# A Trainium2 transformer layer: x^T's first blocks issued from ScalarE's queue, and the first projection chunk run product by product

## The chip, the cores and the metric

The kernel runs on one core of a Trainium2 chip. The metric is the device time of the whole kernel in microseconds (us), the median of several runs. TensorE (PE) does the matrix products, ScalarE (ACT), VectorE (DVE) and GpSimd (POOL) the element work, and DMAs are issued from SyncE's queue (SP) and here, after the change, from ScalarE's queue as well.

## The reference

One layer of a decoder on 256 tokens of width 1024, all in float32: one input projection to 3072 columns, rotary on the first 16 of each head's 64 dims, differential attention (4 heads) and causal attention (8 heads; with 256 tokens the block-sparse group has only its own block), an output projection, LayerNorm, a SwiGLU feed-forward of width 2816, and a second LayerNorm.

```
proj = x @ w_in                              # 256x1024 @ 1024x3072
a = diff_attention(rope(dq), rope(dk), dv);  b = moba_attention(rope(mq), rope(mk), mv)
x = layer_norm(ALPHA * x + concat(a, b) @ w_o)
g, u = split(x @ w_ffn_in)
x = layer_norm(ALPHA * x + (silu(g) * u) @ w_ffn_out)
```

## The kernel before

Every float32 operand of a weight product is split into two parts, hi and lo, and a product runs as three matmuls into one PSUM bank: hi times x's hi, hi times x's lo, lo times x's hi (`mm3`, lines 132 to 134). The weights come as a stream of 1 MB units of four blocks of 128 x 512 (`load_unit`, line 85). ScalarE copies each piece to its hi part (line 96), VectorE subtracts to get the lo part (line 98); of units 2 to 9, GpSimd does one lo piece in four. Five raw buffers, four hi and four lo buffers turn over; x^T's raw tile takes one of the five.

Chunks 0 to 3 of the input projection (`proj_qkT`) give q^T and k^T of the two attention groups, chunks 4 and 5 give the values. Chunk 0 is four column blocks j of 128 columns, each with its own PSUM tile `pj0_j`, over eight contraction blocks k. Its loop runs over k outside and j inside, and each (j, k) is one `mm3`. The four results then go through `rope` (lines 235 to 245), whose shuffles, products and splits are done by VectorE, GpSimd and ScalarE while chunk 1 runs on TensorE. Scores (`scores`, line 271), the combination of the two softmaxes (`diff_combine`, line 296) and transposes (`diff_pt`) are woven into chunks 2 and 3 in the same manner.

At the start, seven matmuls on zeros (`WARM`, line 144) run while the first loads are on their way. x^T (8 blocks of 128 x 256, 128 KB each) and the first unit of w_in (4 blocks of 256 KB) are loaded by eight DMAs, all from SyncE's queue, in an order written by hand (lines 161 and 164); then units 1 to 3 follow in pieces of 256 KB. Each block is split as it arrives (lines 168, 169, 180, 182). The framework that builds the program sorts the instructions of each engine by its own estimate of when they can run, so that the order on an engine is not always that of the source.

Of the kernel before, what the change touches and what calls it, by code (L numbers as in the profile page):

```python
# [11 lines left out]
F32 = mybir.dt.float32  # L12
F32R = mybir.dt.float32r
BF16 = mybir.dt.bfloat16
AF = mybir.ActivationFunctionType
ALU = mybir.AluOpType

P = 128
S = 256
D = 1024  # L20
KT = D // P
# [8 lines left out]
EPS = 1e-5  # L30
WARM = 7  # matmuls on zeros that raise the tensor engine's clock while the first loads run

# weight units loaded / split in more pieces than usual: unit -> pieces
LOAD_PIECES = {1: 4, 2: 4, 3: 4, 4: 4, 5: 4, 6: 2, 7: 2}
SPLIT_PIECES = {16: 4, 17: 4, 18: 4, 19: 4}

# steps of a projection chunk at which attention work is woven in
FIN0, FIN1, FIN2, FIN3 = (20, 24, 28, 31), (4, 6, 8, 10), (5, 4), (5, 2)
SCORES0, SCORES1 = (18, 22, 26, 30), (3, 5, 7, 9)
COMBINE, DIFF_PT = 12, (22, 25, 28, 31)  # L40

# partner of each rotary dim within a 32-partition quadrant
SWAP = [(i + HALF) % 16 if i < 16 else i for i in range(32)]


# The 256 tokens are one key block of the block-sparse group: there is no past block to select, so
# its softmax runs over the own block under the causal mask.
# Weight products: every float32 operand is split exactly into two float32r parts (12 bits each), and
# hi*hi + hi*lo + lo*hi accumulate in PSUM.


@with_exitstack
def hybrid_layer_kernel(ctx, tc, xT, xr, w_in, w_o, w_f1, w_f2, cols, rows, lamb, rot, tri, out):
    nc = tc.nc
# [8 lines left out]

# [1 line left out]
    # unit: [128, 4 blocks, 512] float32, split into two float32r parts  # L65
    units = []
# [11 lines left out]
    raw, hi, lo = {}, {}, {}  # L78
# [26 lines left out]
    def spread(units_, pieces, steps):  # L105
        """Hooks that emit the split of some units evenly over a number of steps."""
        gens = [(u, p) for u in units_ for p in range(pieces)]
        live = {}

        def emit(u):  # L110
            if u not in live:
                live[u] = split_gen(u, pieces)
                state["split"] = u + 1
            next(live[u])

        hooks = {}
        for i, (u, p) in enumerate(gens):
            hooks.setdefault(i * steps // len(gens), []).append(lambda u=u: emit(u))
        return hooks
# [15 lines left out]

# [1 line left out]
    warm = const.tile([P, 512], BF16, name="warm")  # L137
    nc.vector.memset(warm, 0.0)
    tbl = const.tile([P, 2], F32, name="tbl")
    nc.vector.memset(tbl, 0.0)  # L140
    nc.scalar.activation(tbl[:, 1:2], tbl[:, 0:1], AF.Exp)
    wps = psB.tile([P, 512], F32, tag="b", name="wps")
# [16 lines left out]

    def load_x(a, b):  # L160
        nc.sync.dma_start(xTr[:, a:b, :], xT[:, a:b, :])

    def load_w0(i):
        nc.sync.dma_start(raw[0][:, i, :], units[0][:, i, :])

    def split_x(a, b, copy=nc.scalar.copy):
        s = slice(a, b)
        copy(xTh[:, s, :], xTr[:, s, :])  # L168
        nc.vector.tensor_sub(xTl[:, s, :], xTr[:, s, :], xTh[:, s, :].bitcast(F32))

    load_w0(0)
    load_x(0, 1)
    load_x(1, 2)
    load_w0(1)
    load_x(2, 4)
    load_w0(2)
    load_w0(3)
    load_x(4, 8)
    for i in range(4):
        nc.scalar.copy(hi[0][:, i, :], raw[0][:, i, :])  # L180
        split_x(i, i + 1, nc.vector.tensor_copy if i == 0 else nc.scalar.copy)
        nc.vector.tensor_sub(lo[0][:, i, :], raw[0][:, i, :], hi[0][:, i, :].bitcast(F32))
# [23 lines left out]

# [1 line left out]
    apool = axT.enter_context(tc.tile_pool(name="apool", bufs=1))  # L208
    V = [apool.tile([P, 2, 512], F32, name=f"V{i}") for i in range(2)]
    # per pair of 128-row blocks: first token tile in float32, the rest in two float32r parts  # L210
    F0, QH, QL, SH, QA = {}, {}, {}, {}, {}
# [14 lines left out]
    def rope(c, js, ps):  # L226
        """128-row blocks js of q^T or k^T, PSUM -> SBUF, with the rotary part applied."""
        b, m = js[0] // 2, len(js)
        if js[0] % 2 == 0:
            qk_tiles(c, b)  # L230
            SH[c, b] = rpool.tile([P, 2, S], F32, tag="sh", name=f"sh{c}_{b}", bufs=2)
            QA[c, b] = rpool.tile([P, 2, S], F32, tag="qk", name=f"a{c}_{b}", bufs=2)
        bs = slice(js[0] % 2, js[0] % 2 + m)
        sh, a = SH[c, b][:, bs, :], QA[c, b][:, bs, :]
        nc.vector.stream_shuffle(sh, ps, SWAP)
        nc.vector.tensor_mul(a, ps, cos2[:, :m, :])
        nc.gpsimd.tensor_mul(sh, sh, sin2[:, :m, :])
        f, h, l = F0[c, b][:, bs, :], QH[c, b][:, bs, :], QL[c, b][:, bs, :]

        def finish():  # L240
            nc.vector.tensor_add(a, a, sh)
            src = a if c % 2 else a[:, :, P:]
            nc.scalar.copy(h, src)
            nc.vector.tensor_sub(l, src, h.bitcast(F32))
            nc.scalar.copy(f, a[:, :, :P])

        return finish
# [40 lines left out]
    def diff_combine():  # L288
        """E_c0 - lam * (l0 / l1) * E_c1, per query row."""
        sc = small.tile([P, 2, 4], F32, tag="sc", name="sc")  # L290
# [76 lines left out]

# [1 line left out]
    def proj_tok(ps, c, t, k):  # L369
# [4 lines left out]
    def proj_qkT(c, side):  # L374
        """One 512-column chunk, transposed: 128 columns on the partitions, 256 tokens."""
        pool, tag = (psB, "b") if c == 1 else (psA, "acc")
# [5 lines left out]
        bg = spread([1] + [2] if c == 0 else [3, 4, 5] if c == 1 else [2 * c + 2, 2 * c + 3], 4, 28)  # L382
        for n, (j, k) in enumerate(order):
            if n == 16:
# [20 lines left out]
    def proj_v(c, side):  # L405
        """One 512-column chunk for both token tiles."""
        pss = [psA.tile([P, 512], F32, tag="acc", name=f"pj{c}_{t}") for t in range(2)]
# [43 lines left out]

# [1 line left out]
    acc = [[psA.tile([P, 512], F32, tag="acc", name=f"wo{t}_{n}") for n in range(2)] for t in range(2)]  # L453
# [93 lines left out]

# [1 line left out]
    hp = ctx.enter_context(tc.tile_pool(name="hp", bufs=1))  # L549
# [5 lines left out]
    def glu_store(sl, h):  # L555
        """h (float32) -> both parts of h^T."""
        nc.scalar.copy(hTh[sl], h)
        nc.vector.tensor_sub(hTl[sl], h, hTh[sl].bitcast(F32))

    def ffn_rows(c, t, mid=()):  # L560
        """Chunk with tokens on the PSUM partitions; then transposes."""
        ps = psB.tile([P, 512], F32, tag="b", name=f"fr{c}_{t}")
# [54 lines left out]

# [1 line left out]
    acc2 = [[psA.tile([P, 512], F32, tag="acc", name=f"fo{t}_{n}") for n in range(2)] for t in range(2)]  # L619
# [108 lines left out]
```

## Time and profile before

| | |
|---|---|
| median of 3 runs | 319.07 us (318.89 to 320.75) |
| span of the profiled execution, first to last instruction | 317.0 us |
| mean granted TensorE clock | 0.993 of full |
| busy share of the span | PE 96%, PE's weight loads 82%, DVE 71%, ACT 53%, POOL 11% |
| moved by DMA | 57.18 MB, mean 180 GB/s |

The span leaves out what lies before the first and behind the last instruction; the profiled execution has no time of its own beside it, and the median is 2.1 us more than the span. A busy share is an average over the whole span: which engine sets the pace has to be read stretch by stretch. A matmul's record is longer than the distance to the next one, since matmuls are pipelined, so TensorE's speed is read from the distance of two starts.

### The profile page before, as it was taken

The page shows a single profiled execution, that of the slowest core. Times are in us where ns is not written, and L with a number is a line of the kernel's source. Part 1 is how long each engine was busy: PE and PEld are TensorE (multiplying, and loading weights), DVE is VectorE, ACT ScalarE, POOL GpSimd, SP SyncE. Part 2 cuts the span into 40 slices and gives each one's busy share as a digit, 9 for nine tenths or more (in the row PEclk, how much of TensorE's full clock was granted, in tenths as well). Part 3 has the DMA queues.
Part 4 walks back from the last instruction along what each step waited for, and adds up shares of the span by engine and source line. Part 5 has one row for each costly group of instructions (what it writes and reads, how often), then busy time and mean ns, then how long its engine had stood idle before and what let it go on. Part 6 is the DMA issues. An engine that isn't in the chain of part 4 may idle for free.

```text
span 317.0 us, 4689 instructions
## 1 busy us (share of the span) xinstructions
PE 304.6 (96%) x1741; PEld 259.7 (82%) x1741; DVE 224.4 (71%) x437; ACT 169.0 (53%) x349; POOL 36.1 (11%) x38
## 2 busy tenths in 40 slices
PE   7999899999999999999999999999999999999990
PEld 4999789867887788888888888888888888888880
DVE  3799999999977389949386577658657753343275
ACT  3757489398685328247467547646754642422000
POOL 1076553310030010100000000000000000000011
PEclk9999999999999999999999999999999999999997
DMA  6999963444376442659654574475357474000011
GB/s 176 377 305 375 423 236 134 132 135 147 125 254 213 188 136 74 212 247 309 220 172 142 218 254 136 142 267 167 141 224 254 144 266 132 0 2 0 0 66 67
DMA packets 12310, 57.18 MB, mean 180 GB/s; under 512 B 1504, under 2 KB 2272, under 8 KB 6784
## 3 DMA queue, kind: packets, MB, share of 16 engines
q1 hardware_dynamic: 12000, 54.79, 49.5%
q0 software_dynamic: 288, 2.10, 1.9%
q8 instruction: 13, 0.21, 0.3%
q14 instruction: 9, 0.07, 0.1%
HBM read 55.84 MB, written 1.05 MB: 179 GB/s over the span
## 4 chain that ended last, share of the span: by engine, by line
PE 77%; DVE 12%; DMA 4%; issue 3%; POOL 1%; ACT 1%; SPq 1%; DVEq 0%; ACTq 0%
PE fc L590 21%; PE fc L591 11%; PE fo L134 6%; PE fo L132 6%; PE fo L133 6%; DMA raw<-in_w_in_dram 4%; DVE lo L98 4%; PE wo L132 2%; PE fr L133 2%; PE fr L132 2%; PE wo L134 2%; PE wo L133 2%; PE fr L134 2%; PE pj L132 2%; PE pj L134 2%
## 5 line engine op out<-in xcount | busy, mean ns | idle before, releaser
L98 DVE TENSOR_TENSOR lo<-raw,hi 128x1024 fp32r<-128x1024 f32 (+1 forms) x122 | 118.2, 995 | 41.2 <-ACT hi L96 41.1
L96 ACT CAST hi<-raw 128x512 fp32r<-128x512 f32 (+1 forms) x130 | 100.5, 824 | 38.3 <-PE fo L134 19.2
L590 PE MATMUL fc<-x1T,hi 128*128 128x512 f32 x288 | 100.1, 392 | 0.0
L591 PE MATMUL fc<-x1T,lo 128*128 128x256 f32 x288 | 80.7, 280 | 0.0
L590 PEld LDWEIGHTS fc<-x1T,hi 128*128 128x128 f32 x288 | 54.1, 188 | 11.8
L591 PEld LDWEIGHTS fc<-x1T,lo 128*128 128x128 f32 x288 | 54.1, 188 | 0.0
L132 PE MATMUL pj<-xTh,hi 128*128 128x256 f32 x128 | 37.1, 296 | 1.0 <-DVE xTh L168 0.9
L134 PE MATMUL pj<-xTh,lo 128*128 128x256 f32 x128 | 36.2, 289 | 0.7 <-DVE lo L98 0.5
L133 PE MATMUL pj<-xTl,hi 128*128 128x256 f32 x128 | 36.6, 287 | 0.0
L132 PE MATMUL fo<-hi,hTh 128*128 128x512 f32 x82 | 32.4, 395 | 0.0
L133 PE MATMUL fo<-lo,hTh 128*128 128x512 f32 x82 | 32.4, 395 | 0.0
L134 PE MATMUL fo<-hi,hTl 128*128 128x512 f32 x82 | 32.4, 395 | 0.0
L132 PEld LDWEIGHTS pj<-xTh,hi 128*128 128x128 f32 x128 | 24.6, 195 | 2.6 <-ACT hi L180 2.1
L134 PEld LDWEIGHTS pj<-xTh,lo 128*128 128x128 f32 x128 | 24.4, 194 | 1.3 <-DVE lo L98 0.7
L594 DVE TENSOR_TENSOR v<-v,fc 128x256 f32<-128x256 f32 x36 | 15.0, 418 | 14.5 <-ACT v L593 14.5
L133 PEld LDWEIGHTS pj<-xTl,hi 128*128 128x128 f32 x128 | 25.0, 195 | 0.0
L593 ACT COPY v<-fc 128x256 f32<-128x256 f32 x36 | 13.3, 370 | 20.8 <-PE fc L591 20.7
L505 POOL TENSOR_TENSOR rsf<-rsf,mhalf 128x1 f32<-128x1 f32 x2 | 1.8, 924 | 179.3 <-DVE rsf L504 179.3
L134 PEld LDWEIGHTS fo<-hi,hTl 128*128 128x128 f32 x82 | 15.5, 189 | 3.6
L133 PEld LDWEIGHTS fo<-lo,hTh 128*128 128x128 f32 x82 | 15.5, 189 | 3.6
L132 PEld LDWEIGHTS fo<-hi,hTh 128*128 128x128 f32 x82 | 15.5, 189 | 3.5
L98 POOL TENSOR_TENSOR lo<-raw,hi 128x512 fp32r<-128x512 f32 x8 | 13.5, 1689 | 21.3 <-ACT hi L96 21.3
(148 smaller groups left out, 455.8 us busy)
## 6 DMA issues: line engine op xcount, KB each, us to landing
raw<-in_w_f_dram SPq DMA_DIRECT2D x33, 1024.0 KB, 5.2
raw<-in_w_in_dram SPq DMA_DIRECT2D x24, 256.0 KB, 5.4
raw<-in_w_in_dram SPq DMA_DIRECT2D x4, 1024.0 KB, 10.1
raw<-in_w_o_dram SPq DMA_DIRECT2D x4, 1024.0 KB, 4.8
raw<-in_w_in_dram SPq DMA_DIRECT2D x4, 512.0 KB, 7.9
rows<-in_rows_dram POOLq DMA_DIRECT2D x2, 1024.0 KB, 6.9
x_sb<-in_xr_dram SPq DMA_DIRECT2D x1, 1024.0 KB, 10.5
out_dram<-z SPq DMA_DIRECT2D x3, 256.0 KB, 2.1
```

Of the source, the lines that this page charges most:

```text
L96: nc.scalar.copy(h[:, s, :], r[:, s, :])
L98: eng.tensor_sub(l[:, s, :], r[:, s, :], h[:, s, :].bitcast(F32))
L132: nc.tensor.matmul(ps, sh, mh, start=first, stop=False)
L133: nc.tensor.matmul(ps, sh, ml, start=False, stop=False)
L134: nc.tensor.matmul(ps, sl, mh, start=False, stop=last)
L505: nc.gpsimd.tensor_tensor(rs, rs, mhalf[:, :1], op=ALU.pow)
L590: nc.tensor.matmul(ps, hi[u][:, i, ws], x1T[:, k], start=k == 0, stop=False)
L591: nc.tensor.matmul(ps[:, 0, :], lo[u][:, i, ws], x1T[:, k, 0, :], start=False, stop=k == KT - 1)
L593: nc.scalar.copy(v, ps[:, 1, :])
L594: nc.vector.tensor_add(v, v, ps[:, 0, :])
```

## The change

- `WARM` goes from 7 to 9.
- x^T's blocks 0 and 1 are issued from ScalarE's queue, ahead of the first `Exp` that loads its table; the rest stays on SyncE's queue.
- The first weight block is loaded as two halves of 256 columns, and its hi part is made in two halves too.
- The start's splits are written in another order: for block 0, x^T's split on VectorE stands around the weight's; for blocks 1 to 3, x^T's split stands ahead of the weight's.
- Chunk 0 runs, for each k, one product over all four column blocks, then the next product, in place of the three products of one column block after another.

```diff
-WARM = 7  # matmuls on zeros that raise the tensor engine's clock while the first loads run
+WARM = 9
...
-    nc.scalar.activation(tbl[:, 1:2], tbl[:, 0:1], AF.Exp)
...
-    load_w0(0)
-    load_x(0, 1)
-    load_x(1, 2)
+    load_x(nc.scalar, 0, 1)
+    load_x(nc.scalar, 1, 2)
+    nc.scalar.activation(tbl[:, 1:2], tbl[:, 0:1], AF.Exp)
+    load_w0(0, 0, 256)
+    load_w0(0, 256, 512)
     load_w0(1)
-    load_x(2, 4)
+    load_x(nc.sync, 2, 4)
     load_w0(2)
     load_w0(3)
-    load_x(4, 8)
-    for i in range(4):
+    load_x(nc.sync, 4, 8)
+    nc.vector.tensor_copy(xTh[:, 0, :], xTr[:, 0, :])
+    nc.scalar.copy(hi[0][:, 0, :256], raw[0][:, 0, :256])
+    nc.vector.tensor_sub(xTl[:, 0, :], xTr[:, 0, :], xTh[:, 0, :].bitcast(F32))
+    nc.scalar.copy(hi[0][:, 0, 256:], raw[0][:, 0, 256:])
+    nc.vector.tensor_sub(lo[0][:, 0, :], raw[0][:, 0, :], hi[0][:, 0, :].bitcast(F32))
+    for i in range(1, 4):
+        split_x(i, i + 1)
         nc.scalar.copy(hi[0][:, i, :], raw[0][:, i, :])
-        split_x(i, i + 1, nc.vector.tensor_copy if i == 0 else nc.scalar.copy)
         nc.vector.tensor_sub(lo[0][:, i, :], raw[0][:, i, :], hi[0][:, i, :].bitcast(F32))
...
-        for n, (j, k) in enumerate(order):
+        for k in range(KT if c == 0 else 0):
+
+            u, i = k // 4, k % 4
+            for p, (w, x) in enumerate(((hi, xTh), (hi, xTl), (lo, xTh))):
+                if 4 * k + p == 16:
+                    ahead(1, splits=-1)
+                for f in bg.get(4 * k + p, []) + (bg.get(4 * k + 3, []) if p == 2 else []):
+                    f()
+                for j in range(4):
+                    nc.tensor.matmul(pss[j][:, 0, :], w[u][:, i, j * P : (j + 1) * P], x[:, k, :],
+                                     start=(k, p) == (0, 0), stop=(k, p) == (KT - 1, 2))
+        for n, (j, k) in enumerate(order if c else ()):
```

On SyncE's queue (SP) the start's DMAs stood in this order before (xTr is x^T, raw_101 the first weight unit, raw_139 the next; the sizes are partitions x elements):

```order
L164 DMA raw_101<-in_w_in_dram 128x512
L161 DMA xTr<-in_xT_dram 128x256 x2
L164 DMA raw_101<-in_w_in_dram 128x512
L161 DMA xTr<-in_xT_dram 128x512
L164 DMA raw_101<-in_w_in_dram 128x512 x2
L161 DMA xTr<-in_xT_dram 128x1024
L85 DMA raw_139<-in_w_in_dram 128x512 x4
```

and stand in this one now (raw_102 is the first weight unit, raw_143 the next):

```order
L160 DMA xTr<-in_xT_dram 128x512
L163 DMA raw_102<-in_w_in_dram 128x256 x2
L163 DMA raw_102<-in_w_in_dram 128x512 x3
L160 DMA xTr<-in_xT_dram 128x1024
L85 DMA raw_143<-in_w_in_dram 128x512 x4
```

The built order differs from the source's: x^T's blocks 2 and 3 (128 x 512) have moved to the head of SyncE's queue, ahead of all weights, while blocks 0 and 1 are on ScalarE's queue.

ScalarE's first instructions now (before, it had the table load, the activation, and then casts of weights and x^T in turn, a weight first):

```order
L160 DMA xTr<-in_xT_dram 128x256 x2
L172 ACT_TABLE_LOAD
L172 ACTIVATE tbl<-tbl 128x1
L167 CAST xTh<-xTr 128x256 x2
L181 CAST hi_103<-raw_102 128x256
L167 CAST xTh<-xTr 128x256
L183 CAST hi_103<-raw_102 128x256
L187 CAST hi_103<-raw_102 128x512 x3
```

The two issues stand ahead of the table load, and the first weight cast stands behind the casts of x^T's blocks 1 and 2.

On VectorE, some 50 us into the program, where the last score block (s_3) is turned into E and the combination of the softmaxes (`sc`, then eight products into E) follows, before:

```order
L235 STREAM_SHUFFLE sh_1_744<-pj_1_520 128x512
L236 TENSOR_TENSOR a_1_745<-pj_1_520,cs_sb 128x512
L98 TENSOR_TENSOR lo_754<-raw_521,hi_753 128x512
L241 TENSOR_TENSOR a_1_745<-a_1_745,sh_1_744 128x512
L291 RECIPROCAL rl_518<-ls_517 128x16
L292 TENSOR_TENSOR sc<-ls_517,rl_518 128x8
L98 TENSOR_TENSOR lo_754<-raw_521,hi_753 128x512
L244 TENSOR_TENSOR l_1_743<-a_1_745,h_1_742 128x256
L293 TENSOR_SCALAR sc<-sc,nlam 128x8
L98 TENSOR_TENSOR lo_754<-raw_521,hi_753 128x512
L296 SCALAR_TENSOR_TENSOR E_514<-E_514,sc 128x128
```

and now:

```order
L241 STREAM_SHUFFLE sh_1_748<-pj_1_524 128x512
L242 TENSOR_TENSOR a_1_749<-pj_1_524,cs_sb 128x512
L297 RECIPROCAL rl_522<-ls_521 128x16
L247 TENSOR_TENSOR a_1_749<-a_1_749,sh_1_748 128x512
L298 TENSOR_TENSOR sc<-ls_521,rl_522 128x8
L98 TENSOR_TENSOR lo_758<-raw_525,hi_757 128x512 x2
L250 TENSOR_TENSOR l_1_747<-a_1_749,h_1_746 128x256
L299 TENSOR_SCALAR sc<-sc,nlam 128x8
L98 TENSOR_TENSOR lo_826<-raw_613,hi_825 128x512
L302 SCALAR_TENSOR_TENSOR E_518<-E_518,sc 128x128
```

Of unit raw_521 (now raw_525) three lo pieces stood behind the first shuffle product; now its first one stands eight rows further up, ahead of the last score block, and a piece of the next unit (raw_613) has come ahead of the products into E. TensorE's own order changes in chunk 0 alone.

## Rows read from the trace of the kernel before

**Rows 1.** The page: the chain of work that ended last, by engine.

```profile
PE 77%; DVE 12%; DMA 4%; issue 3%; POOL 1%; ACT 1%; SPq 1%; DVEq 0%; ACTq 0%
```

**Rows 2.** Busy time of each engine by stretch, then granted clock, DMA share, GB/s.

```profile
...
6.00:8.00 2.00, 2.00 (x11) 2.00 (x11) 1.05 (x3) 0.62 (x1) 0.00 (x0) 1.00 0.76 155
8.00:12.00 4.00, 3.82 (x27) 3.54 (x27) 2.12 (x4) 2.53 (x6) 0.00 (x0) 1.00 1.01 361
12.00:17.00 5.00, 5.00 (x44) 5.00 (x43) 4.53 (x8) 4.78 (x10) 0.84 (x1) 1.00 1.05 395
17.00:40.00 23.00, 21.80 (x179) 20.75 (x178) 23.00 (x56) 13.35 (x33) 14.60 (x13) 1.00 0.99 368
40.00:71.00 31.00, 30.04 (x225) 26.33 (x224) 30.89 (x88) 23.62 (x72) 11.32 (x7) 1.00 0.45 158
71.00:300.00 229.00, 228.96 (x1199) 192.50 (x1200) 150.69 (x255) 121.58 (x230) 6.13 (x6) 1.00 0.48 166
...
```

**Rows 3.** The chain that ended last, in order of time: start us, us, what.

```profile
...
3.54 6.54 DMA raw<-in_w_in_dram
10.09 6.01 DMA raw<-in_w_in_dram
...
16.77 1.31 DVE lo L98
...
```

**Rows 4.** Waits from 12 to 75 us: total us, times, longest us.

```profile
...
PE ppd L279 <- DVE E L296: 0.6, 1, 0.6
...
PE pj L134 <- DVE lo L98: 0.5, 1, 0.5
...
```

**Rows 5.** Timeline of the start: start us, us, instruction, idle time before it.

```profile
...
0.73 1.28 ACT L141 ACT_TABLE_LOAD   x1 [0.73 <-PEq L718]
...
1.18 0.89 SPq L161 DMA_DIRECT2D xTr<-in_xT_dram  x2
...
1.19 3.17 PE L144 MATMUL wps<-warm 128*128 128x512 bf16 x7 [1.19 <-DVE tbl L140]
...
3.61 0.62 ACT L180 CAST hi<-raw 128x512 fp32r<-128x512 f32 x1 [1.38 <-DMA raw<-in_w_in_dram]
...
5.23 1.20 PE L132 MATMUL pj<-xTh,hi 128*128 128x256 f32 x4 [0.87 <-DVE xTh L168]
...
6.12 0.62 ACT L180 CAST hi<-raw 128x512 fp32r<-128x512 f32 x1 [0.28 <-DMA raw<-in_w_in_dram]
...
8.16 0.42 PE L133 MATMUL pj<-xTl,hi 128*128 128x256 f32 x1
...
8.38 0.42 PE L132 MATMUL pj<-xTh,hi 128*128 128x256 f32 x1
...
8.59 0.71 ACT L168 CAST xTh<-xTr 128x256 fp32r<-128x256 f32 x2 [1.85 <-DMA xTr<-in_xT_dram]
...
9.06 0.28 PE L132 MATMUL pj<-xTh,hi 128*128 128x256 f32 x1
...
9.18 0.28 PE L133 MATMUL pj<-xTl,hi 128*128 128x256 f32 x1
...
10.11 0.39 PE L132 MATMUL pj<-xTh,hi 128*128 128x256 f32 x1 [0.18 <-ACT hi L180]
...
12.08 1.29 DVE L169 TENSOR_TENSOR xTl<-xTr,xTh 128x512 fp32r<-128x512 f32 x2 [0.64 <-ACT xTh L168]
...
```

**Rows 6.** Timeline around the end of chunk 0, same columns.

```profile
...
18.09 0.45 DVE L235 STREAM_SHUFFLE sh<-pj 128x256 f32<-128x256 f32 x1
...
18.43 0.68 DVE L98 TENSOR_TENSOR lo<-raw,hi 128x512 fp32r<-128x512 f32 x1
...
18.83 0.28 PE L134 MATMUL pj<-xTh,lo 128*128 128x256 f32 x1
...
```

**Rows 7.** Timeline of VectorE and TensorE around the combination, same columns.

```profile
...
56.02 3.73 DVE L296 SCALAR_TENSOR_TENSOR E<-E,sc 128x128 f32<-128x128 f32 x8
...
65.47 0.39 PE L133 MATMUL s<-l,h 64*128 64x256 f32 x1 [0.26 <-DVE l L244]
...
```

More of the change, by code (lines that the diff above doesn't have):

```diff
@@ L158, in hybrid_layer_kernel, with load_x, load_w0 @@
     lo[0] = wlo.tile([P, 4, 512], F32R, tag="lo", name="lo0")
[L160 to L164, printed above, removed]
+    def load_x(eng, a, b):
+        eng.dma_start(xTr[:, a:b, :], xT[:, a:b, :])
+    def load_w0(i, a=0, b=512):
+        nc.sync.dma_start(raw[0][:, i, a:b], units[0][:, i, a:b])
     def split_x(a, b, copy=nc.scalar.copy):
```

## The prediction

> **What bounds the kernel now.** Three views, in this order. The page's chain gives TensorE 77% of the span, VectorE 12% and DMA 4% [rows 1]; these are averages over the kernel, so I split the span by stretch. From 71 to 300 us TensorE is busy 228.96 of 229 us: nothing waits there except on TensorE itself. From 17 to 40 us it is VectorE that is full, 23.00 of 23.00 us, and from 40 to 71 us it has 30.89 of 31; TensorE has 21.80 and 30.04 there, so it idles a little in both [rows 2]. From 12 to 17 us VectorE has 4.53 of 5.00. The chain in order of time says what stands ahead of that: DMAs of the first weights, from 3.54 over 10.09 to 16.1 us, and then VectorE's lo piece at 16.77 us [rows 3]. So three stages follow one another: DMA to 16 us, VectorE to about 71 us, TensorE to the end. The change touches only the first 19 us of TensorE's work and the first DMAs. TensorE itself is not late in that stretch: it waits for VectorE at the lo pieces (0.5 us) and at the products into E (0.6 us) [rows 4]. Whatever TensorE gains before that, it gives back at these waits, unless VectorE comes earlier too; and VectorE comes earlier only if the DMAs do.
>
> What "time" is here: the median of 319.07 us is 2.1 us more than the profiled span of 317.0 us. I make the sum on the span and carry the 2.1 us along, that is, I add it to 319.07. A change of 1% is 3.2 us; less than that this kernel's runs can hardly tell from nothing.
>
> **The DMA stream.** Two of SyncE's issues go to ScalarE's queue: 0.89 us for the two [rows 5]. One comes back, since the first weight block is loaded in halves. So SyncE issues the later pieces some 0.45 us sooner, and x^T's first blocks leave beside SyncE's first DMA instead of behind it. This pays only where the issue is what is waited for. The stretches say that it is not: the DMA engines are 76% busy from 6 to 8 us, and full from 8 us on (1.01, then 1.05) [rows 2]. Up to 10.11 us the same 1.28 MB must have come in either kernel, and up to the piece that VectorE waits for at 16.77 us the same 3.9 MB. The gain is therefore at most the 0.45 us, and at least nothing, as far as the issue goes. There is one odd place, though: from 6 to 8 us only 155 GB/s come in, against 361 and 395 in the next two stretches [rows 2]. If another order of the first DMAs did away with it, some 0.41 MB would come that much sooner: (361 - 155) x 2 us, or 1.05 us at 395 GB/s. Nothing in the rows says that the order is its cause. Halving the first block's rows to 1 KB costs on the other side; x^T's blocks 0 and 1 are such transfers already, so I allow 0.2 us. I take 0.3 us of gain, nearer to the issue's end, and keep -1.1 and +0.2 as bounds.
>
> The Trainium skill (DMA: Bandwidth & Descriptors, section on issuing engines not being separate DMA queues) says that DMAs started from several engines run on the same 16 DMA engines, and that a second issuer saves only the issue time. By that rule this term would be 0 to -0.45 us, and the rest of the gain would not exist; the DMA share of 1.01 and 1.05 agrees with it.
>
> **The first product.** It starts at 5.23 us [rows 5]. What it needs is x^T's block 0 and the first weights. In the built order x^T's blocks 2 and 3 lead SyncE's queue, so 640 KB go out up to the first half block (128 + 128 + 256 + 128) where it was 384 KB. By the arrivals before, 256 KB at 3.61 us and 768 KB at 6.12 us [rows 5], 640 KB is 3.61 + 2.51 x 384/512 = 5.5 us. ScalarE's cast of a half block takes about half of its 0.62 us, and its casts of x^T's blocks 1 and 2 stand ahead in its queue; so the first product starts at about 5.9 us, 0.7 us later than before. The next weight block is then the 1024th KB, which came at 8.59 us (x^T's blocks 2 and 3 [rows 5]), so block k = 1 starts near 9.2 us. Block k = 2 needs the 1280th KB as before, and started at 10.11 us on a wait for ScalarE's cast of it [rows 5]. There the two kernels meet again: k = 0 and k = 1 are 24 matmuls, and the 0.7 us and the later k = 1 are swallowed if these 24 are through by about 10.1 us.
>
> That hangs on TensorE's speed. The granted clock reads 1.00 in all these stretches [rows 2], but starts of 256-column matmuls are 0.22 us apart at 8.16 and 8.38 us and 0.12 us at 9.06 and 9.18 us [rows 5]: 1.2 GHz first, 2.4 GHz behind. Before the rise lay the seven matmuls on zeros (1.19 us on, 3.17 us), an idle 0.87 us, and products without a break from 5.23 us on. With nine they last 2 x 0.43 us longer (3.17/7 is 0.45, with the last one's tail), to about 5.2 us, and the idle time ahead of the first product stays near 0.7 us. At 2.4 GHz the 24 take 24 x 0.12 = 2.9 us, at 1.2 GHz 24 x 0.21 = 5.1 us. With k = 1 from 9.2 us on, the first is 10.4 us (its lo piece on VectorE, 0.68 us by [rows 6], and then four matmuls come last) and the second 9.2 + 12 x 0.21 = 11.7 us: 0.3 us late or 1.6 us late.
>
> The Trainium skill (TensorE: Matmul & The Clock Gate, section on what is actually happening) states that the throttled clock is the default and activity releases it, which speaks for two more matmuls on zeros. The rise after unbroken work at 5.23 us agrees; no run here shows what nine give.
>
> **Who notices.** Chunk 0 ends at 18.83 + 0.28 = 19.1 us, and VectorE's first shuffle of it started at 18.09 us, when VectorE was free [rows 6]. Now that shuffle stands behind one more lo piece (0.68 us [rows 6]), and the four column blocks end together within four matmuls, which puts the first one's end 0.3 to 0.7 us nearer to the chunk's. So 0.3 us late costs VectorE nothing, and 1.6 us late costs it 1.6 - 0.7 + 0.3 = 1.2 us, on the path. I take 0, since the clock should be up by then and k = 2 sets the pace; bounds 0 and +1.2. Nothing below zero, because TensorE's earlier end only meets the waits of [rows 4]. The loop itself (product by product) changes no count: 96 matmuls, as many weight loads.
>
> **Cover.** ScalarE's two issues, 0.89 us at SyncE's price [rows 5], push its table load (1.28 us from 0.73 us) to 1.6 us, and it is ready by 3.2 us; its first cast before was at 3.61 us on a wait for a DMA [rows 5]. Hidden. If the first DMA landed before 3.2 us, it would cost the difference, some tenths. The casts and subtractions of the start are the same work in another order; VectorE waits there in any case (0.64 us ahead of 12.08 us for x^T's last blocks [rows 5]).
>
> **The new order at 50 us.** One more lo piece (0.68 us) ahead of the products into E, which take 3.73 us from 56.02 us [rows 7] and for the first of which TensorE waits [rows 4]. It is taken from behind them, so TensorE's next wait for VectorE, 0.26 us at 65.47 us [rows 7], shrinks. Between nothing and 0.7 us; I take 0.3, the half that the wait at 65.47 us can give back.
>
> **Sum.** -0.3 (DMA) + 0 (first product) + 0 (ScalarE's queue) + 0.3 (order at 50 us) = 0: 319.1 us, with -1.1 + 0 and +0.2 + 1.2 + 0.7 as the corners: 318.0 to 321.2.
>
> **Rivals.**
> - The slow place at 6 to 8 us goes away with the new order, and VectorE starts its full stretch earlier. For it: VectorE is idle ahead of 12.08 us and would follow at once. Against: no row ties the place to the order. It gives 319.07 - 1.05 = 318.0, or 0.2 us less if the order at 50 us brings something back.
> - Slower: x^T's blocks 2 and 3 ahead of the weights make k = 0 and k = 1 late, TensorE runs them at 1.2 GHz, and VectorE waits for chunk 0's end. It decides from 0.4 us of lateness at k = 2 on. For it: the built queue order, and an idle gap ahead of the first product in which the clock may stay low. Against: k = 2 waits for its weights in any case. 319.07 + 1.2 + 0.3 = 320.6.
> - TensorE bounds the start after all, and the clock's earlier rise counts in full: 18 matmuls between 5.23 and 9 us at 0.12 instead of 0.21 us, 1.6 us, so 317.4. Against: VectorE's 23.00 of 23.00 us.
> - The change does not do what it says: with x^T's blocks 2 and 3 ahead, the weights do not start beside block 0, and nothing moves: 319.1, the forecast's own number.
>
> **How the numbers follow.** Forecast (with the last rival) 0.5, slow place gone 0.2, late weights 0.2, TensorE's clock 0.05, other 0.05. The forecast's own range is 318.5 to 319.8; with the two rivals at its sides taken in, 317.7 to 320.6. More than 1% either way needs 3.2 us. Faster by that much would need VectorE's full stretch to start 3 us earlier, at 9 us, when x^T's last blocks have not come (VectorE waited for their cast up to 12.08 us [rows 5]): 0.04. Slower by it would need several of the bounds at once: 0.03. So 0.93 within 1%.
>
> **What would show it.** Right: VectorE's full stretch starts at 12 us within 0.5 us, and it is still busy in all of 17 to 40 us; the first product comes at about 5.9 us; chunk 0 ends near 19 us; TensorE's wait for the products into E grows from 0.6 towards 1.1 us. Wrong: x^T's last blocks land a microsecond earlier, or VectorE stands idle ahead of its first shuffle, or TensorE's products after 71 us have gaps of their own.

## The result, and the profile after

The changed kernel is slower: 324.02 us median of 4 runs (323.56 to 324.14), beside 319.91 us of the kernel before in the same set of runs (4 runs, 318.89 to 320.87). The ratio is 1.0141, 95% interval 1.0105 to 1.0177: 4.5 us, 3.4 to 5.7. A second measurement in the course of the experiments gave 1.0128 (1.0095 to 1.0160). Both times, 324.02 and 322.38 us, lie above the range of the prediction and above its upper corner of 321.2. The four runs of the kernel before lie two and two, 1.8 us apart; what parts the runs of one program is shown below.

The profiled execution has a span of 322.3 us, 5.3 more than before. First the stretches, columns as in [rows 2]: the span's part, then PE, PEld, DVE, ACT and POOL busy, granted clock, DMA share, GB/s.

```profile
4.40:7.80 3.40, 1.71 (x10) 1.03 (x8) 2.51 (x7) 2.52 (x7) 0.00 (x0) 1.00 1.06 391
7.80:11.20 3.40, 3.40 (x19) 3.40 (x18) 2.94 (x5) 1.97 (x5) 0.00 (x0) 0.50 0.84 233
...
17.00:40.00 23.00, 21.59 (x176) 20.81 (x174) 21.11 (x51) 10.57 (x26) 13.17 (x12) 1.00 1.00 362
40.00:71.00 31.00, 28.58 (x227) 25.58 (x226) 29.61 (x82) 22.85 (x69) 11.20 (x7) 1.00 0.44 157
71.00:76.00 5.00, 3.26 (x18) 2.42 (x19) 5.00 (x18) 3.96 (x14) 0.27 (x1) 1.00 0.40 121
76.10:79.40 3.30, 3.30 (x16) 2.17 (x14) 3.30 (x14) 2.91 (x14) 0.00 (x0) 0.50 0.28 119
79.50:300.00 220.50, 220.50 (x1153) 185.67 (x1154) 144.08 (x232) 117.58 (x211) 5.75 (x6) 1.00 0.48 167
```

Three things differ from [rows 2]. The granted clock is 0.50 twice, from 7.8 to 11.2 us and from 76.1 to 79.4 us: TensorE at 1.2 GHz there, at 2.4 GHz (1.00) in the other rows. VectorE, full before from 17 to 40 us (23.00), now has 21.11 there, and 29.61 in place of 30.89 in the stretch behind. And from 71 to 76 us, where TensorE had no gap at all, it is busy 3.26 of 5.00 us. The last row says where to stop looking: from 79.5 us on nothing is lost any more.

The start in the timeline, columns as in [rows 5]:

```profile
0.74 0.38 SPq L160 DMA_DIRECT2D xTr<-in_xT_dram  x1
1.18 2.31 SPq L163 DMA_DIRECT2D raw<-in_w_in_dram  x5
1.19 3.67 PE L143 MATMUL wps<-warm 128*128 128x512 bf16 x9 [1.19 <-DVE tbl L140]
...
1.66 1.28 ACT L172 ACT_TABLE_LOAD   x1 [1.66 <-PEq L735]
...
4.87 0.41 ACT L167 CAST xTh<-xTr 128x256 fp32r<-128x256 f32 x1 [1.72 <-DMA xTr<-in_xT_dram]
...
6.00 0.40 ACT L181 CAST hi<-raw 128x256 fp32r<-128x256 f32 x1
...
6.45 1.12 PE L398 MATMUL pj<-xTh,hi 128*128 128x256 f32 x4 [1.58 <-ACT hi L181]
```

SyncE's first DMA is x^T's blocks 2 and 3. The first product starts at 6.45 us, 1.22 later than in [rows 5], after TensorE stood idle for 1.58 us; the fall of the clock follows it. The end of chunk 0 is then late for VectorE, which comes early. VectorE's timeline, and under it TensorE's last products of the chunk:

```profile
16.01 1.82 DVE L98 TENSOR_TENSOR lo<-raw,hi 128x512 fp32r<-128x512 f32 x2 [0.66 <-ACT hi L96]
19.72 0.01 DVE L241 LOAD_MASK_SELECT sh<-pj  x1 [1.89 <-PE pj L398]
19.72 0.45 DVE L241 STREAM_SHUFFLE sh<-pj 128x256 f32<-128x256 f32 x1
...
19.40 0.63 PE L398 MATMUL pj<-xTh,lo 128*128 128x256 f32 x4
```

The lo piece that VectorE had at 16.77 us [rows 3] it has at 16.01 us, so the DMA stream did gain, 0.76 us; but its first shuffle goes from 18.09 [rows 6] to 19.72 us, 1.63 later, behind 1.89 us of waiting. That explains less than half of the 5.3 us. TensorE's waits from 12 to 80 us, columns as in [rows 4], show the rest:

```profile
PE s L132 <- DVE negm L277: 1.7, 1, 1.7
PE ppd L285 <- DVE E L302: 1.5, 1, 1.5
```

The wait for E has grown from 0.6 to 1.5 us, and at the top is one that the kernel before did not have. It is at the third pair of scores of the second group. Two rows of the kernel before and four of after, TensorE's timeline:

```profile
69.87 0.40 PE L134 MATMUL pj<-hi,xTl 128*128 128x512 f32 x1
70.20 0.38 PE L132 MATMUL s<-h,h 64*128 64x256 f32 x1
```

```profile
72.18 0.40 PE L134 MATMUL pj<-hi,xTl 128*128 128x512 f32 x1
74.32 0.35 PE L132 MATMUL s<-h,h 64*128 64x256 f32 x1 [1.74 <-DVE negm L277]
...
76.16 0.63 PE L134 MATMUL pj<-hi,xTl 128*128 128x512 f32 x1
76.59 0.63 PE L132 MATMUL pj<-hi,xTh 128*128 128x512 f32 x1
```

These scores take the PSUM buffer of the first pair, and get it when VectorE has read that (the two lines L277, `E` and `negm`). VectorE in the kernel after, ahead of these lines:

```profile
66.67 0.69 DVE L250 TENSOR_TENSOR l<-a,h 128x512 fp32r<-128x512 f32 x1
67.88 1.29 DVE L98 TENSOR_TENSOR lo<-raw,hi 128x512 fp32r<-128x512 f32 x2 [0.51 <-ACT hi L96]
...
69.10 0.74 DVE L241 STREAM_SHUFFLE sh<-pj 128x512 f32<-128x512 f32 x1
...
72.94 0.28 DVE L277 CUSTOM_DVE_ANT_0 E<-s,mask 128x128 f32<-128x128 f32 x1
...
73.15 0.68 DVE L250 TENSOR_TENSOR l<-a,h 128x512 fp32r<-128x512 f32 x1
73.75 0.41 DVE L277 CUSTOM_DVE_ANT_0 E<-s,mask 128x256 f32<-128x256 f32 x1
```

Two lo pieces (1.29 us, and 0.51 us of waiting for ScalarE's hi) stand between l and the shuffle, and an l line of 0.68 us between the two E lines, after which the buffer is free. In the kernel before:

```profile
64.74 0.67 DVE L244 TENSOR_TENSOR l<-a,h 128x512 fp32r<-128x512 f32 x1
...
65.35 0.73 DVE L235 STREAM_SHUFFLE sh<-pj 128x512 f32<-128x512 f32 x1
...
69.20 0.28 DVE L271 CUSTOM_DVE_ANT_0 E<-s,mask 128x128 f32<-128x128 f32 x1
...
69.41 0.41 DVE L271 CUSTOM_DVE_ANT_0 E<-s,mask 128x256 f32<-128x256 f32 x1
```

The shuffle followed l at once, and the two E lines each other; from l to the second E line it was 4.67 us, and now it is 7.08. None of these lines is touched by the diff: the scheduler put them in another order.

How late the same instruction is in the profile of after: first product +1.22, lo piece -0.76, first shuffle +1.63, the score that stood at 65.47 us [rows 7] +2.51 (67.98), the one at 70.20 us +4.12, the end of the span +5.3 us. From that last score to the end it is 246.8 us before and 248.0 now: by these two profiles the second fall of the clock costs 1.2 us.

### The profile page after: what moved, and what is told of

Same layout as the page of the kernel before. It is cut to its first block, busy times and chain, and to the rows that moved or that the text cites. A ratio compares the mean times of both kernels' runs of the same rounds, so it can differ in the third digit from the quotient of the medians.

```text
span 322.3 us, 4693 instructions
## 1 busy us (share of the span) xinstructions
PE 305.8 (95%) x1743; PEld 260.4 (81%) x1743; DVE 225.5 (70%) x437; ACT 169.3 (53%) x350; POOL 34.9 (11%) x38
## 4 chain that ended last, share of the span: by engine, by line
PE 74%; DVE 10%; DMA 8%; issue 2%; POOL 2%; ACT 1%; SPq 0%; DVEq 0%; ACTq 0%; POOLq 0%
PE fc L607 21%; PE fc L608 10%; DMA raw<-in_w_in_dram 7%; PE fo L134 6%; PE fo L132 6%; PE fo L133 6%; DVE lo L98 3%; PE wo L132 2%; PE fr L133 2%; PE fr L132 2%; PE wo L134 2%; PE wo L133 2%; PE fr L134 2%; PE pj L132 2%; PE pj L134 2%
## 5 line engine op out<-in xcount | busy, mean ns | idle before, releaser
L134 PE MATMUL pj<-xTh,lo 128*128 128x256 f32 x96 | 27.3, 285 | 1.4 <-DVE lo L98 0.8
L132 PE MATMUL pj<-xTh,hi 128*128 128x256 f32 x96 | 27.8, 289 | 0.0
L133 PE MATMUL pj<-xTl,hi 128*128 128x256 f32 x96 | 27.0, 281 | 0.0
L134 PEld LDWEIGHTS pj<-xTh,lo 128*128 128x128 f32 x96 | 18.1, 188 | 2.0 <-DVE lo L98 1.2
L132 PEld LDWEIGHTS pj<-xTh,hi 128*128 128x128 f32 x96 | 18.1, 188 | 0.5
L133 PEld LDWEIGHTS pj<-xTl,hi 128*128 128x128 f32 x96 | 18.1, 188 | 0.0
```

The lines of the kernel that those rows point to most:

```text
L132: nc.tensor.matmul(ps, sh, mh, start=first, stop=False)
L133: nc.tensor.matmul(ps, sh, ml, start=False, stop=False)
L134: nc.tensor.matmul(ps, sl, mh, start=False, stop=last)
```

## The experiments

Two theories at the outset. **A**: the start and the order are two separate losses, and the order, which the scheduler changed on VectorE and ScalarE from 31 us on, is the larger. **B**: the start is the loss; the order only follows the lateness. A third question was the loop by itself. Microseconds below are the ratio's excess times the median of the kernel before in the same set of runs, with its interval.

**The order undone, and the order alone.** In both kernels the issue order of VectorE and ScalarE is fixed from the first a = a + sh of chunk 0 on, by edges that set the order of issue and add no wait. The first is the changed kernel with the old order, the second the kernel before with the new one.

```diff
+        for eng, (count, ranks) in ORDER.items():
+            own = [i for i in nc.cur_bb.bb.instructions if i.engine == getattr(mybir.EngineType, eng)]
...
+            for p, q in zip(ranks, ranks[1:]):
+                tc.add_manual_dep(own[q], own[p].name, mybir.DependencyInfo(
+                    mybir.DependencyClass.NoSync, mybir.DependencyReason.DATA), reason="order")
```

> The changed kernel with one thing put back: from the first addition of the rotary parts (a = a + sh of chunk 0) on, VectorE and ScalarE issue in the order of the kernel before. Two theories for the 4.4 us lost. Theory A (start and order both): the late start (first product +1.22 us, TensorE at half clock from 7.80 to 11.21 us, VectorE idle 1.89 us before the first shuffle) is worth about 1.4 us, and the new order downstream the rest, with the 2.14 us wait at 74 us and the second fall of the clock: 1.0 to 2.0 us above the kernel before, about 321.4, and no fall of the clock near 76 us. Theory B (start alone; the order only follows the lateness): about as slow as the changed kernel, 323.5 to 324.5.

> The kernel before, its start and loop untouched, but VectorE and ScalarE forced into the changed kernel's order from the first addition of the rotary parts on. Theory A: the order alone costs 2 to 3.5 us, 322 to 323.5, the wait of TensorE for VectorE's E lines at about 58 us grows from 0.6 to about 1.2 us, and a wait near 71 us of over 1.5 us shows with a fall of the clock behind it. Theory B: within 0.7 us of the kernel before, about 320.

Measured: 320.24 us for the first (12 runs), ratio 1.0017 (0.9992 to 1.0041), +0.5 us (-0.3 to +1.3). The second 322.46 us (6 runs), 1.0116 (1.0092 to 1.0140), +3.7 us (2.9 to 4.5); its largest waits, and the stretch behind them:

```profile
PE s L175 <- DVE negm L314: 1.7, 1, 1.7
PE ppd L322 <- DVE E L339: 1.5, 1, 1.5
```

```profile
73.30:76.60 3.30, 3.30 (x11) 2.27 (x9) 3.30 (x18) 2.91 (x14) 0.00 (x0) 0.50 0.63 263
```

With no change at the start, the new order alone shows both waits and the second fall of the clock. Theory B falls: of the 4.1 to 4.5 us the order costs 3.7. Theory A holds in kind, but it had put 1.0 to 2.0 us on the start and 2 to 3.5 on the order. The runs of the first kernel fell on two levels, five at 318.2 to 318.4 and seven at 320.2 to 320.4 us; more on that below.

**The loop.** The changed kernel with the old loop, and the kernel before with the new one.

```diff
-        for k in range(KT if c == 0 else 0):
...
-        for n, (j, k) in enumerate(order if c else ()):
+        for n, (j, k) in enumerate(order):
```

> The changed kernel with the loop of chunk 0 as it was before (three products of a block and k together); all loads, splits and the order of VectorE, ScalarE and GpSimd are those of the changed kernel. If the product-by-product loop costs something by itself, it is that all four blocks end within the last four matmuls, so that the first shuffle starts only 0.03 us before the chunk's end, where it started 0.74 us before it in the kernel before: then 0.4 to 0.8 us less than the changed kernel, about 323.4. If the loop is not the cause, 324.0 and the same clock rows. If the loop is what made the start late (products that wait for a part not yet there), 2 us less or more.

> The kernel before with the product-by-product loop alone; loads and splits as before, the order of VectorE but for one lo line ahead of the first shuffle as before too. If the loop costs by its late ends alone: 0.4 to 0.8 us above the kernel before, about 320.5. If it costs nothing: 319.9. If the loop is the main loss: 322 or more.

Measured: 321.92 us (4 runs), 1.0108 (1.0094 to 1.0122), +3.4 us; and 318.79 us (12 runs), 1.0010 (0.9998 to 1.0023), +0.3 us (-0.1 to +0.7). In the kernel before, the loop alone costs little or nothing. In the changed kernel, undoing it brings back 0.6 to 1.1 us by the ratios (1.0108 against 1.0128 and 1.0141), which their intervals don't tell from nothing. The median is 2.1 us under the first 324.02, but the profile of the old loop has no fall of the clock at the start, and the changed kernel's own runs without that fall lie at 322.1 to 322.6 us (last set). Whether the loop has a part in that fall, four runs don't tell. The built orders tell where the new one comes from: with the old loop VectorE and ScalarE keep the changed kernel's order to the instruction, and with the new loop alone they keep the old one but for one lo piece. It is the loads and splits of the start that made the scheduler order them anew.

**The two stretches of the order.** The kernel before, with the new order in one stretch only. The late one on VectorE, as built, the old order and under it the new one (lo10 in pieces, `l`, `sh`, `a` of chunk 3, E the score lines):

```diff
-lo10[0] l_0 sh_1 a_1 lo10[1] a_1 lo10[2] E E l_1 E E lo10[3] ...
+l_0 lo10[0] lo10[1] sh_1 a_1 lo10[2] a_1 lo10[3] E l_1 E E E lo11[0] ...
```

> The kernel before with one stretch alone in the changed kernel's order: VectorE from the pieces of lo10 around l of chunk 3 to the scores of the second group, and ScalarE's hi10, hi11, h and f lines there (64 to 77 us); everything ahead of it as before. If the stretch is what makes TensorE wait for VectorE's negm line at 70 us, and the wait what takes its clock down: a wait of 1.2 to 1.7 us there, half clock for about 3.4 us behind it, and 2.0 to 2.6 us above the kernel before in all, about 321. If the wait only comes about because VectorE is already late from the reordering at 33 to 60 us: no wait over 0.5 us, no fall, within 0.5 us of the kernel before.

> The mirror image: the kernel before with VectorE's order of the changed kernel from 31 to 63 us alone (l_1 and sh_1 of chunk 1; the lo8 and lo9 pieces that go ahead of the last scores and of the E lines) and ScalarE's hi8 ahead of h and f there; from l of chunk 3 on as before. If the two stretches add up: 1.0 to 1.6 us above the kernel before (320 to 320.4), TensorE's wait for E at 58 us grown from 0.6 to about 1.5 us, no fall of the clock near 74 us. If only the late stretch counts: 0 to 0.4 us.

Measured: late 321.60 us (11 runs), 1.0067 (1.0043 to 1.0091), +2.1 us; early 319.75 us (12 runs), 1.0030 (1.0007 to 1.0054), +1.0 us. Of the late one a wait and a stretch, of the early one a wait and two stretches:

```profile
PE s L175 <- DVE negm L314: 2.1, 1, 2.1
```

```profile
73.10:76.40 3.30, 3.30 (x11) 2.26 (x12) 3.30 (x17) 2.91 (x15) 0.00 (x0) 0.50 0.48 201
```

```profile
PE ppd L322 <- DVE E L339: 1.5, 1, 1.5
```

```profile
11.60:14.70 3.10, 3.10 (x17) 3.10 (x17) 2.49 (x6) 3.05 (x6) 0.00 (x0) 0.51 1.05 402
...
76.00:80.00 4.00, 4.00 (x25) 3.04 (x24) 4.00 (x19) 3.13 (x15) 0.00 (x0) 1.00 0.59 238
```

Each stretch brings its own wait without the other, and 2.1 + 1.0 is near to the 3.7 us of both. The late wait doesn't need a VectorE that is already late.

Two things limit the profiles. That of the early order is one of its two slow runs (321.66 us; ten of the twelve lie at 319.1 to 320.1), and it has a fall of the clock at the start, from 11.6 us, ahead of every row that was put in another order. And the late order's runs lie in two groups: five at 320.2 to 320.9 us with a mean granted clock of 0.992 to 0.993, six at 321.6 to 322.4 with 0.987 to 0.989, of which the profile is one. 3.3 us at half clock lower the mean by 0.005. So the fall seems to follow the wait in about half of the runs; the wait alone would then cost 1.9 us and the fall 1.2 more. No profile of the lower group shows it, and a fall at the start would lower the mean as much.

**The wait filled.** The changed kernel, with work for TensorE just ahead of the wait.

```diff
+        if (g, j) == (1, FILL_AT):
+            for _ in range(FILL):
+                nc.tensor.matmul(state["acc"], warm[:, :P], warm, start=False, stop=False)
```

> The changed kernel, its order kept, with seven products of zeros added to the V projection's sum just ahead of the scores at which TensorE waits 2.14 us at 72 us (they add nothing to the result and need 1.5 us of TensorE). If it is the idle time that takes the clock down: the full clock goes on past 76 us, the wait is 0.3 to 0.7 us, and the kernel is 1.0 us faster than the changed one (323.0, 1.011 of the kernel before). If the fall has another cause: 324.0 and a fall near 76 us all the same. If TensorE was not free in that time: slower by up to 1.5 us.

Measured: 320.95 us (8 runs), 1.0077 (1.0047 to 1.0107), against 1.0128 and 1.0141. In its profile:

```profile
70.63 1.69 PE L312 MATMUL pj<-warm 128*128 128x512 bf16 x7
72.53 0.35 PE L176 MATMUL s<-h,h 64*128 64x256 f32 x1 [0.21 <-DVE negm L324]
```

```profile
74.00:80.00 6.00, 6.00 (x33) 4.62 (x33) 5.28 (x26) 5.17 (x23) 0.00 (x0) 1.00 0.37 123
```

VectorE frees the buffer no sooner for it; the scores still wait, 0.21 us. But the clock stays at 2.4 GHz, so the fall came of the idle time. That is not one profile's luck: the runs lie on two levels here too (the start, below), and the five at the lower one have a mean granted clock of 0.990 to 0.996, the four of the changed kernel there (last set) 0.988 to 0.989. It is worth a little more than the 1.0 us expected: the lower level is 320.6 to 321.0 here and 322.1 to 322.6 in the changed kernel, 1.1 to 2.0 us apart, in two sets whose kernels before are 0.2 us apart; the two profiles at that level have spans of 319.0 and 320.3 us.

**The two levels of the start.** The changed kernel with the old order, the first kernel of the experiments, with 16 warm matmuls; all else in the same order.

```diff
-WARM = 9
+WARM = 16
```

> The first kernel of the study (changed start and loop, old order downstream) with 16 warm matmuls in place of 9, all else in the same order. Its runs fell on two levels, 318.2 and 320.3 us. If the two come of the 1.6 us in which TensorE has nothing to do between the warm matmuls and the first product, after which its clock is up in some runs and down in others: with the gap filled all runs lie at the lower level, 318.2, a median 0.5 us under the kernel before, and the profile has the clock up from the warm matmuls on. If the levels come of the loads or of the profile's chance: two levels again. If the warm matmuls delay the first product: 0.3 us or more above the lower level.

Measured: 318.45 us, 12 runs from 318.2 to 319.1, ratio 0.9983 (0.9966 to 1.0000). The two levels are gone. TensorE's rows at the start, of the kernel with 9 and then of that with 16:

```profile
1.19 4.02 PE L186 MATMUL wps<-warm 128*128 128x512 bf16 x9 [1.19 <-DVE tbl L183]
6.42 1.41 PE L441 MATMUL pj<-xTh,hi 128*128 128x256 f32 x4 [1.21 <-ACT hi L224]
...
8.48 1.05 PE L441 MATMUL pj<-xTh,lo 128*128 128x256 f32 x4
9.34 1.05 PE L441 MATMUL pj<-xTh,hi 128*128 128x256 f32 x4
```

```profile
1.19 6.32 PE L199 MATMUL wps<-warm 128*128 128x512 bf16 x16 [1.19 <-DVE tbl L196]
7.16 0.82 PE L454 MATMUL pj<-xTh,hi 128*128 128x256 f32 x4
```

With 9 the profiled run (of the upper level) has a gap and then slow products: from 8.48 to 9.34 us four starts are 0.21 us apart each, the pace of 1.2 GHz in the kernel before. (The granted clock reads 1.00 there, as it did in [rows 2] beside the same pace.) With 16 the gap is closed, the products start 0.74 us later, four run in 0.82 us, and the kernel is at the lower level all the same.

The changed kernel itself, profiled once at 324.14 us (above) and once at 322.16 (last set), shows the two levels in one program. Of the second profile the stretches in which the first has 0.50:

```profile
7.80:11.20 3.40, 3.40 (x31) 3.40 (x29) 2.64 (x5) 2.05 (x5) 0.00 (x0) 1.00 0.90 224
74.00:77.30 3.30, 3.30 (x16) 2.32 (x14) 3.30 (x15) 2.91 (x15) 0.00 (x0) 0.51 0.36 151
```

From 7.80 to 11.20 us it has 31 products where the slower run has 19; the fall at 74 us is in both. So whether TensorE runs chunk 0's first products at 2.4 or at 1.2 GHz decides between two times that lie 2.0 us apart. The slow pace comes in two ways, a clock that rises and falls again (the changed kernel) and one that has not risen yet (the kernel with the old order, above). The kernel with the old order and 16 warm matmuls is the best of the versions run, but 0.5 us (0 to 1.1) under the kernel before is hardly to be told from it.

**Controls: the changed kernel again, the kernel before with 16 warm matmuls, SyncE's queue in the order of the program, and one queue.** The third has x^T's blocks 2 and 3 behind the first two weight blocks; the fourth issues x^T's blocks 0 and 1 from SyncE as well. Both have the old order and 16 warm matmuls, and k = 1's splits ahead of those of k = 2 and 3, which the kernel with 16 above has not. The fourth's change of the loads:

```diff
-    load_x(nc.scalar, 0, 1)
-    load_x(nc.scalar, 1, 2)
...
     load_w0(0, 256, 512)
+    load_x(nc.sync, 0, 1)
+    load_x(nc.sync, 1, 2)
```

> The changed kernel itself once more, beside the next three and the kernel before, to have its distance with more runs: 1.014 of the kernel before, about 323.3 if the kernel before runs at 318.8. If its start falls on two levels as that of the first kernel of the study, its runs spread over 2 us.

> The kernel before with 16 warm matmuls in place of 7 and nothing else (VectorE's, ScalarE's and GpSimd's order held). Control for the kernel with the changed start, the old order and 16 warm matmuls (0.9983 of the kernel before): if that one owes its 0.3 us and its single level to the filled gap alone, this one reaches the same, 318.3 to 318.5, and no run at 320.4 or above. If it owes them to the earlier loads: no faster than the kernel before, 318.8, or slower, since the warm matmuls now stand ahead of a first product that could start at 5.2.

> Changed start and loop, old order downstream, 16 warm matmuls, and on SyncE's queue x^T's blocks 2 and 3 behind the first two weight blocks, as the program is written (in the changed kernel they were issued first). If their place cost the late first product: the first weight half lands at 4.9 us in place of 5.4, the first split is done by 5.9, and chunk 0 ends 0.3 to 0.5 us earlier where the warm matmuls allow it: 318.1, 0.3 us under the same kernel without this. If chunk 0's end is set by the last blocks (x^T 4 to 8 lands at 9.4 us, lo of the later blocks from VectorE): no difference, 318.45.

> As the kernel beside it, but x^T's blocks 0 and 1 on SyncE's queue too, behind the first weight block: no load is issued from ScalarE. If two queues bring the start forward: the blocks land 0.4 to 0.9 us later here, and chunk 0 ends 0.3 us later or more (318.7). If the queue doesn't matter, since the loads share the same DMA engines and later blocks set chunk 0's end: no difference, 318.3 to 318.5.

Measured: the changed kernel 322.38 us (6 runs), 1.0128 (1.0095 to 1.0160); four runs at 322.1 to 322.6, two at 323.9 and 324.0, the two levels again. At either level it lies 3.7 to 3.9 us above the kernel with the old order (318.2 to 318.4 and 320.2 to 320.4), so the order's price, across these two sets of runs, does not hang on the start. The other three:

| kernel | median us | ratio | interval |
|---|---|---|---|
| before, 16 warm matmuls | 320.08 | 1.0044 | 1.0026 to 1.0062 |
| changed start, SyncE in order | 318.84 | 1.0006 | 0.9991 to 1.0021 |
| the same, one queue | 319.40 | 1.0019 | 1.0002 to 1.0036 |

The kernel before with 16 warm matmuls missed: they cost it 1.4 us, and its runs spread from 318.9 to 321.6. Its first product waits behind them (6.83 us in its profile, 5.23 in [rows 5]), and yet its profiled run is the fastest, 318.85; what the others lose stays open. Sixteen do more than fill the gap here, so this shows only that they bring nothing without the earlier loads.

SyncE in order missed too: ScalarE has its first weights at 3.16 us, where the changed kernel's first cast of any kind came at 4.87 us, and the first shuffle comes at 18.32 us against 18.59 in the kernel with 16 warm matmuls above, but the time is no better. Its chain shows what sets chunk 0's end (start us, us, what):

```profile
2.58 6.44 DMA raw<-in_w_in_dram
...
9.04 0.63 ACT hi L251
...
9.71 8.57 PE pj L462 x69
```

The product at 9.71 us is the first of k = 2, and it waits for the third weight block's load and cast; from there on the chain is 69 products in a row, to 18.3 us. So k = 2's weights and TensorE's own work behind them set the end. One queue lies above both times that were expected of it, with its first shuffle at 18.49 us, 0.17 later; where the rest of its time goes stays open. One queue against two: 0.6 us by the medians, with intervals that overlap; not settled.

## Why the prediction was wrong

**The step that failed is "the new order at 50 us"**, taken as 0.3 us with bounds 0 and +0.7. The order on VectorE and ScalarE cost 3.7 us. I had weighed one of the places where it changes, the lo piece ahead of E. That stretch (31 to 63 us) measured 1.0 us (0.2 to 1.7). The place at 64 to 74 us was left out of the sum, and measured 2.1 us (1.4 to 2.9): a wait of 1.7 to 2.1 us and, in its profile, 3.3 us at half clock behind it. That from 71 to 300 us "nothing waits there except on TensorE itself" was true of the rows and false as an argument. The score at 70.20 us took a buffer that VectorE's line from 69.41 us had freed, 69.82 by its length, so the slack was 0.4 us. In the new order four lo10 pieces instead of three stand ahead of the first E line, and an l line between the two: 0.68 + 0.67 us by the rows of before, less 0.4 of slack, 0.95 us of wait that could have been worked out. The rest is VectorE's wait of 0.51 us for ScalarE's hi10, which the new order puts behind h and f, and the clock.

**DMA, -0.3 us** with bounds -1.1 and +0.2: right in kind. x^T's last blocks were cast at 9.38 us in place of 11.43, and the lo piece came 0.76 us earlier. The slow place went from 6 to 8 us (now 391 GB/s from 4.4 to 7.8) to 7.8 to 11.2 us (233 GB/s): part of the first rival came true and brought no time by itself, since VectorE then waited for TensorE.

**The first product, 0 us, "since the clock should be up by then"**: the reason was wrong, the size by chance near. It came at 6.45, not 5.9 us: ScalarE's two casts of x^T stand ahead of the half block's, and the second waits for its load. In the first profile the clock rose during the warm matmuls (nine in 3.67 us, against 4.02 in the other profiles with nine) and fell again after the gap. Where TensorE is slow behind the gap the start costs what the second rival said in kind (TensorE at 1.2 GHz, VectorE waiting for chunk 0's end), 2.0 us between the levels and not 1.2; where it isn't, the kernel with the old order runs at 318.2 to 318.4, under the median of 318.7 of the kernel before. Over all its runs the start is +0.5 us (-0.3 to +1.3), and the forecast of -0.3 lies at the edge of that interval. That k = 2 sets the pace was wrong for the changed kernel as well: in its faster profile k = 2 starts at 9.78 us without a wait, and TensorE's own 96 products run on to 18.3 us; with SyncE's queue in order k = 2 does wait, to 9.71 us.

**ScalarE's queue, 0 us**: right. The table load moves to 1.66 us and is done at 2.94; the first cast waits for a DMA until 4.87 us. **The loop, 0 us**: right by the loop alone, +0.3 us (-0.1 to +0.7); the 0.6 to 1.1 us of undoing it are not told from nothing. The Trainium skill (DMA: Bandwidth & Descriptors, section on issuing engines not being separate DMA queues) gave a second issuer at most its issue time; the controls agree so far as they tell: 0.6 us between one queue and two, not apart by their intervals.

**The chances.** Slower by over 1% had 0.03, because it would "need several of the bounds at once". It needed none of them: the bound of the order was too narrow. All three signs of being wrong showed: x^T's last blocks 2.05 us earlier, VectorE idle ahead of its first shuffle for 1.89 us, and gaps in TensorE's work after 71 us.

## What to carry to other kernels

An edit at the head of a scheduled kernel is also an edit of everything behind it that the scheduler places: compare the built order of every engine to its end, and price each moved row against the slack of the buffer or operand that it frees. A stage that shows no gap has no loss in it, but it may have a slack of 0.4 us, and only the order tells what is about to use it up. To change one thing, hold the order of the rest; here that alone turned +4.5 us into +0.5 us.

## What was not expected of the hardware

The granted clock fell behind a single idle stretch of 1.7 us (2.1 us from start to start), with work at 2.4 GHz before and behind it: 0.50 from 76.1 to 79.4 us, and the 512-column products were 0.43 us apart in place of 0.23. The wait of 1.48 us for E at 60.4 us, in the same profile, had no fall behind it, and by the late order's two groups of runs the longer one may not have it each time. Seven products of zeros in the idle time kept it at 1.00 and were worth 1.1 to 2.0 us by the lower levels of the two kernels. The Trainium skill (TensorE: Matmul & The Clock Gate, section on what is actually happening) calls the throttled clock the default that activity releases; that the idle stretch here was followed by half clock, and the filled one was not, agrees with it.

At the start the same program takes either way. Behind 1.2 to 1.6 us of idle time between warm matmuls and first product the profiles show TensorE at 2.4 GHz from 7.8 us on (322.16 us) or at 1.2 GHz to 11.2 us (324.14 us); of the twelve runs of the kernel with the old order, five lie at one level and seven at the other, 2.0 us apart.

With x^T's blocks 2 and 3 first on SyncE's queue, beside x^T's block 0 on ScalarE's, ScalarE had nothing to cast before 4.87 us; with the half weight block first it cast at 3.16 us. Why the first casts are 1.7 us apart stays open. The kernel gained nothing from it. Landings move without any change of the loads, too: the kernel before with the new order, whose start is the same, has its first product at 4.38 us in its profile, 0.85 us ahead of [rows 5], so single profiles tell the start only within that.
